# One table preload in the convolution's norm, its steps spaced by one microsecond more, and the sample attention begun at other groups

## The chip, the cores and the metric

The kernel runs on one core of a Trainium2 chip. Five engines work side by side, each through its own list of instructions in order: TensorE (PE, with its weight loads as PEld), VectorE (DVE), ScalarE (ACT), GpSimd (POOL) and SyncE (SP), whose list here is almost only DMA issues. They wait for each other through semaphores. The metric is the device time of one execution in microseconds (us); lower is better.

## The reference

One step of a one-layer streaming encoder, all in f32, for 1024 prompt frames and 32 sample frames (1056 tokens). What matters here:

```
u  = rmsnorm(x) @ w_in                       # gives GLU input, q, k, v, forget logits, two gates
cu = a * sigmoid(gl)                         # GLU
cy = silu(layernorm(depthwise_conv31(cu))) @ w_conv_pw
ao = attend(q, k, v, logf) @ w_attn_o        # softmax(q k^T / 8 + decay), causal, 8 heads of 64
mixed = sigmoid(g_conv) * cy + sigmoid(g_attn) * ao
h  = x + mixed @ w_out
h  = h + (silu(z @ w_gate) * (z @ w_up)) @ w_down,  z = rmsnorm(h)
y  = rmsnorm(h)
```

The prompt attends to itself in 8 query blocks of 128 rows. The 32 sample frames attend to 1024 cached keys and to themselves.

## The kernel before

All activations stand feature by token: a tile has 128 features on the partitions and the 1056 tokens in three chunks of 352 columns. Each f32 operand is split into a high and a low part, so a product of a weight block with a chunk is three matmuls for each of the 128-row steps of the contraction (`products`, line 429). Weight blocks come in by DMA (`raw`), ACT writes the high part (line 245), POOL or DVE the low part (line 248).

**The middle of the program (about 250 to 663 us)** is one long list of PE products, the dense products of line 429 (k, q, v, then the gates, then in `mixers` the convolution's pointwise product), into which the attention is woven. Every four dense matmuls `tick` advances a planner's clock (`plan.pe`) and lets a set of Python generators (threads) put their next piece into the PE list when the planner's clock has reached the time that they yielded. The order on PE is therefore the order of the program text; the tile framework's scheduler orders ACT, DVE, POOL and SP in this region by priority and dependence. The threads are

- `score_thread`, `transpose_thread`, `value_thread`: 32 groups (4 head pairs `p`, 2 heads `hh`, 4 groups `g` of 256 query rows), each with scores (line 1073), softmax (DVE 1080, ACT exp 1083, DVE 1085), transposes of the probabilities (PE 1095, ACT 1102, DVE 1104) and the value product (PE 1112);
- `norm_conv`: the layer norm of the convolution's output, four accumulators of 128x1056, with its sums on PE (line 786), `Ln` on ACT (815), `Exp` (820), `Tanh` (839), and at the end the split operands written to a DRAM scratch `ccd`;
- `sample_thread`: two halves (heads 0 to 3, heads 4 to 7) of the sample attention, `sample_attention(u)`. Each loads the cached keys (`kr`) and values (`vr`) and the decay rows (`ls`) on SP's queue, transposes the keys on PE (line 251), and makes scores (1241, 1243), softmax (1245 to 1249), transposes and value products (1274, 1275), whose results DVE copies to `os` (1278). A half begins when the transposes of so many groups are in the list: 30 for the first half, 28 for the second.

PSUM: the scores have one buffer (`ps`), the transposes, the norm's sums and the sample attention share two banks (`pt`).

**The handover at 663 us.** After `mixers` all tiles of this region are given up and `tokens_in_pairs` lays new pools over the same memory. `attn_out` then issues its loads on SP in this order: `o` for two column blocks (line 1442), the gate `gd` of three output blocks for the first two column blocks (line 1450), `o` for the other two, the `md` of the three blocks, `gd` and `md` of the second half, and then the next two weight blocks `raw` of `w_attn_o` (line 1393). The first product blocks 0 and 1 have their weights already; block 2 needs the first of these `raw` loads. Each load into a new tile waits until the last user of the old tile in that place is done.

Of the kernel before, what the change touches and what calls it, by code (L numbers as in the profile page):

```python
# [37 lines left out]
N_C = 55  # L38
SLACK = 0.65
LOOK = 1  # L40
LATE = 6

CONV_RATE, FORGET_RATE, NORM_RATE = 0.5, 0.25, 0.35
# [20 lines left out]
def f32(ap):  # L64
    return ap.bitcast(F32)
# [75 lines left out]
class Builder:  # L141
# [227 lines left out]
    def jobs(self):  # L369
# [4 lines left out]
        for t in range(4):  # L374
            win(512 + P * t)
            win(P * t)
        assert LATE <= 8
        gates = [(s, j) for s in range(2) for j in range(8)]
        self.early, self.late = gates[:16 - LATE], gates[16 - LATE:]
        gate = lambda s, j: win((W_GC, W_GA)[s] + P * j)  # L380
# [396 lines left out]
    def norm_conv(self):  # L777


        nc, acc, plan = self.nc, self.acc, self.plan  # L780
        self.acc = None
        cs = lambda c: slice(CH * c, CH * c + CH)

        def summed(a, c):
            ps = self.pst()
            nc.tensor.matmul(ps[:, :CH], self.ones, a[:, cs(c)], start=True, stop=True)
            return ps[:, :CH], plan.on_pe(0.62)

        yield plan.pe
        a = self.U([T], s="ln")  # L790
        for t in range(1, 4):
            nc.vector.tensor_add(a, acc[0] if t == 1 else a, acc[t])
            e = plan.on_dve(plan.pe, 1.3)
            yield plan.pe + 2.0
        for c in range(NCH):
            yield max(plan.ready(e), plan.t_next())
            ps, at = summed(a, c)
            for t in range(4):
                nc.vector.scalar_tensor_tensor(acc[t][:, cs(c)], ps, -1.0 / DC, acc[t][:, cs(c)], op0=ALU.mult,
                                               op1=ALU.add)  # L800
            plan.t_used(plan.on_dve(at, 2.1))
            yield plan.pe + 4.0
        a, b = self.U([T], s="ln"), self.U([T], s="sq")
        for t in range(4):
            nc.scalar.activation(b if t else a, acc[t], AF.Square)
            e = plan.on_act(plan.pe, 1.2)
            if t:
                nc.vector.tensor_add(a, a, b)
                e = plan.on_dve(e, 1.3)
            yield plan.pe + 3.0  # L810
        r = b
        for c in range(NCH):
            yield max(plan.ready(e), plan.t_next())
            ps, at = summed(a, c)
            nc.scalar.activation(r[:, cs(c)], ps, AF.Ln, bias=self.eps_ln, scale=1.0 / DC)
            nc.scalar.activation(a[:, cs(c)], ps, AF.Identity, bias=self.eps_ln, scale=1.0 / DC)
            plan.t_used(plan.on_act(at, 1.1))
            yield plan.pe + 2.0

        nc.scalar.activation(r, r, AF.Exp, scale=-0.5)  # L820
        plan.on_act(plan.pe, 1.2)
        yield plan.pe + 2.0
        nc.vector.scalar_tensor_tensor(a, a, -0.5, r, op0=ALU.mult, op1=ALU.mult)
        plan.on_dve(plan.pe, 1.3)
        yield plan.pe + 2.0
        nc.vector.tensor_mul(a, a, r)
        plan.on_dve(plan.pe, 1.3)
        yield plan.pe + 2.0
        nc.vector.scalar_tensor_tensor(r, a, 1.5, r, op0=ALU.add, op1=ALU.mult)
        plan.on_dve(plan.pe, 1.3)  # L830
        del a, b
        yield plan.pe + 2.0
        for t in range(4):
            nc.vector.scalar_tensor_tensor(acc[t], acc[t], self.g("ln_g", t), r, op0=ALU.mult, op1=ALU.mult)
            plan.on_dve(plan.pe, 1.3)
            yield plan.pe + 3.0

            th = self.U([T], s="sg")
            nc.scalar.activation(th, acc[t], AF.Tanh, bias=self.lnb2[:, t:t + 1], scale=0.5)
            nc.scalar.activation(acc[t], acc[t], AF.Identity, bias=self.g("ln_b", t))  # L840
            plan.on_act(plan.pe, 2.3)
            yield plan.pe + 3.0
            nc.vector.scalar_tensor_tensor(acc[t], th, 1.0, acc[t], op0=ALU.add, op1=ALU.mult)
            plan.on_dve(plan.pe, 1.3)
            yield plan.pe + 2.0
            hi, lo = self.U([T], FR, "cch"), self.U([T], FR, "ccl")
            nc.scalar.activation(hi, acc[t], AF.Copy, scale=0.5)
            nc.vector.scalar_tensor_tensor(lo, acc[t], 0.5, f32(hi), op0=ALU.mult, op1=ALU.subtract)
            plan.on_dve(plan.on_act(plan.pe, 1.1), 1.3)
            for i, x in enumerate((hi, lo)):  # L850
                nc.sync.dma_start(self.ccd[t, i], f32(x))
            acc[t] = th = hi = lo = None
            yield plan.pe + 3.0


    def forget_products(self):
# [176 lines left out]
    def attention(self):  # L1033
        nc = self.nc
# [93 lines left out]
        N, plan = len(items), self.plan  # L1128
        o_free = [0.0]
        loaded, probs, pt_ready, pts, done = {}, {}, {}, {}, {"t": 0, "v": 0}  # L1130

        def score_thread():
            for n in range(N):
                p, hh, g = items[n]
                while not (self.c_done and self.ready.get(p)) or n > done["t"] + LOOK:
                    yield None
# [50 lines left out]

        def sample_thread():
            for u in range(2):
                while done["t"] < (30, 28)[u] or not self.ready.get(2 * u + 1):  # L1190
                    yield None
                yield from self.sample_attention(u)

        self.norm = Thread(self.norm_conv())
        self.threads = [Thread(x()) for x in (value_thread, transpose_thread, score_thread, sample_thread)] + [self.norm]

    def sample_attention(self, u):

        nc, I = self.nc, self.I
# [17 lines left out]
                                    channel_multiplier=1)  # L1217
        plan = self.plan
        vr_at = 0.0
        yield plan.pe + 6.0  # L1220
        kT = []
        for i in range(2):
            kT.append(self.U([NP], s="kT"))
            for s in range(2):
                yield plan.t_next()
                t = self.pst()
# [27 lines left out]
        for a in range(2):  # L1254
            yield max(plan.ready(e), plan.t_next())
            t = self.pst()
# [6 lines left out]
        t = self.pst()  # L1263
# [859 lines left out]
```

## Time and profile before

| | |
|---|---|
| median of 3 runs | 1569.53 us (1568.97 to 1569.88) |
| the profiled execution | 1572.19 us |
| its span from the first to the last instruction | 1570.4 us |
| PE busy | 1513.8 us, 96% of the span |
| mean granted TensorE clock | 0.985 of full speed |

The profiled execution is 1.79 us longer than its span (launch and end), and 2.66 us longer than the median of the runs. In the rows below `<-` before an engine name is what ended an idle time; `pd<-cch,wlo` names the output and the inputs of an instruction without buffer numbers; x3 means three instructions in a row.

### The profile page before, as it was taken

The page shows a single profiled execution, that of the slowest core. Times are in us where ns is not written, and L with a number is a line of the kernel's source. Part 1 is how long each engine was busy: PE and PEld are TensorE (multiplying, and loading weights), DVE is VectorE, ACT ScalarE, POOL GpSimd, SP SyncE. Part 2 cuts the span into 40 slices and gives each one's busy share as a digit, 9 for nine tenths or more (in the row PEclk, how much of TensorE's full clock was granted, in tenths as well). Part 3 has the DMA queues.
Part 4 walks back from the last instruction along what each step waited for, and adds up shares of the span by engine and source line. Part 5 has one row for each costly group of instructions (what it writes and reads, how often), then busy time and mean ns, then how long its engine had stood idle before and what let it go on. Part 6 is the DMA issues. An engine that isn't in the chain of part 4 may idle for free.

```text
span 1570.4 us, 27321 instructions
## 1 busy us (share of the span) xinstructions
PE 1513.8 (96%) x10622; PEld 1477.1 (94%) x10622; DVE 957.5 (61%) x1743; ACT 593.2 (38%) x1219; POOL 482.1 (31%) x482
## 2 busy tenths in 40 slices
PE   8999999989999999988998999999999999999997
PEld 7999998979999998888997999999999999999996
DVE  7799998668776566355797544444444444234236
ACT  4411212375655444233543333333333342122115
POOL 2200000433432212310000655565555553122222
PEclk9999999999999999989999999999999999999999
DMA  8312232434633467856854222222222237223213
GB/s 251 120 41 81 87 100 75 132 76 134 203 105 112 119 208 223 266 185 184 262 151 159 82 80 70 71 75 82 82 82 82 82 102 232 83 79 112 84 63 111
DMA packets 212880, 193.54 MB, mean 123 GB/s; under 512 B 13018, under 2 KB 185846, under 8 KB 212751
## 3 DMA queue, kind: packets, MB, share of 16 engines
q1 hardware_dynamic: 212015, 189.91, 39.6%
q8 instruction: 83, 1.36, 0.4%
q0 software_dynamic: 576, 1.62, 0.3%
q14 instruction: 46, 0.38, 0.1%
q10 hardware_dynamic: 160, 0.27, 0.0%
HBM read 135.08 MB, written 56.68 MB: 122 GB/s over the span
## 4 chain that ended last, share of the span: by engine, by line
PE 65%; DVE 6%; ACT 3%; issue 3%; DMA 2%; POOL 1%; SPq 0%; DVEq 0%; ACTq 0%; POOLq 0%
PE pd L1736 26%; PE pd L1430 18%; PE pd L429 11%; PE po L1112 2%; PE ps L1073 2%; PE pt L1095 2%; PE pd L1899 1%; PE pt L251 1%; DVE gate L1495 1%; DMA xt<-xT 1%; DVE h L1659 1%; DVE ml L1499 1%; PE pd L1924 1%; DVE wlo L1418 1%; PE pt L1274 0%
## 5 line engine op out<-in xcount | busy, mean ns | idle before, releaser
L1736 PE MATMUL pd<-zh,whl 128*128 128x264 f32 x2464 | 455.6, 286 | 10.5 <-ACT t L1740 9.6
L1736 PEld LDWEIGHTS pd<-zh,whl 128*128 128x128 f32 x2464 | 386.3, 190 | 11.5 <-ACT t L1740 10.1
L1736 PE MATMUL pd<-zl,whl 128*128 128x264 f32 x1232 | 352.4, 286 | 0.0
L429 PE MATMUL pd<-xl,whi 128*128 128x352 f32 x832 | 270.6, 325 | 0.5 <-POOL xl L539 0.5
L429 PE MATMUL pd<-xh,whi 128*128 128x352 f32 x832 | 271.0, 326 | 0.0
L429 PE MATMUL pd<-xh,wlo 128*128 128x352 f32 x832 | 270.9, 326 | 0.0
L1736 PEld LDWEIGHTS pd<-zl,whl 128*128 128x128 f32 x1232 | 234.3, 190 | 0.0
L1726 DVE TENSOR_TENSOR t<-pd,t 128x264 f32<-128x264 f32 x176 | 75.4, 429 | 202.1 <-POOL t L1744 154.1
L248 POOL TENSOR_TENSOR whl<-ws,whl 128x512 fp32r<-128x512 f32 x105 | 135.6, 1292 | 147.9 <-ACT whl L245 147.9
L429 PEld LDWEIGHTS pd<-xl,whi 128*128 128x128 f32 x832 | 156.8, 188 | 2.0 <-POOL xl L539 0.8
L429 PEld LDWEIGHTS pd<-xh,whi 128*128 128x128 f32 x832 | 156.8, 188 | 1.4
L429 PEld LDWEIGHTS pd<-xh,wlo 128*128 128x128 f32 x832 | 156.8, 188 | 0.7
L766 DVE SCALAR_TENSOR_TENSOR acc<-cu,wdw,acc 128x1024 f32<-128x1024 f32 x120 | 147.3, 1284 | 0.2
L1875 DVE TENSOR_TENSOR h<-pd,h 128x352 f32<-128x352 f32 x96 | 49.7, 523 | 138.3 <-PE pd L1430 138.2
L1430 PE MATMUL pd<-hl,whi 128*128 128x352 f32 x360 | 116.1, 323 | 0.0
L1430 PE MATMUL pd<-hh,whi 128*128 128x352 f32 x360 | 116.1, 322 | 0.0
L1430 PE MATMUL pd<-hh,wlo 128*128 128x352 f32 x360 | 116.1, 322 | 0.0
L245 ACT CAST whl<-ws 128x512 fp32r<-128x512 f32 x115 | 71.4, 621 | 74.7 <-DVE ws L1705 72.1
L248 POOL TENSOR_TENSOR wlo<-raw,whi 128x1024 fp32r<-128x1024 f32 (+1 forms) x31 | 63.9, 2062 | 100.3 <-ACT whi L245 84.7
L245 ACT CAST whi<-raw 128x1024 fp32r<-128x1024 f32 (+1 forms) x47 | 45.0, 957 | 112.0 <-PE pd L429 79.2
L1418 POOL TENSOR_TENSOR wlo<-raw,whi 128x640 fp32r<-128x640 f32 x24 | 39.4, 1643 | 131.9 <-ACT whi L1417 117.0
L1743 POOL TENSOR_TENSOR t<-t,t 128x264 f32<-128x264 f32 x44 | 34.0, 773 | 146.3 <-ACT t L1740 146.3
(349 smaller groups left out, 3061.1 us busy)
## 6 DMA issues: line engine op xcount, KB each, us to landing
raw<-in_w_in SPq DMA_DIRECT2D x35, 512.0 KB, 4.0
hidd<-y SPq DMA_DIRECT2D x43, 264.0 KB, 2.0
hid<-hidd SPq DMA_DIRECT2D x18, 528.0 KB, 4.5
gd<-gate SPq DMA_DIRECT2D x48, 176.0 KB, 1.8
q<-qd SPq DMA_DIRECT2D x32, 256.0 KB, 5.0
raw<-in_w_down SPq DMA_DIRECT2D x24, 320.0 KB, 3.3
raw<-in_w_gate SPq DMA_DIRECT2D x13, 512.0 KB, 4.9
raw<-in_w_up SPq DMA_DIRECT2D x13, 512.0 KB, 4.7
```

The lines of the kernel that those rows point to most:

```text
L245: nc.scalar.copy(hi, src)
L248: (lo_engine or nc.gpsimd).tensor_tensor(lo, src, f32(hi), ALU.subtract)
L429: nc.tensor.matmul(ps[:, :n], lhs, b, start=(m == 0), stop=(m == total - 1))
L766: nc.vector.scalar_tensor_tensor(acc[:, 0:NP], cu[:, j:j + NP], w(j), acc[:, 0:NP], op0=ALU.mult, op1=ALU.add)
L1073: nc.tensor.matmul(s[:, 512 * j:512 * j + e - o], q[:, m, qs], k[:, o:e], start=(m == 0), stop=(m == 1))
L1095: nc.tensor.transpose(t[:, o:o + P], lt[n, b][:, P * kb:P * kb + P], self.ident)
L1418: low = lambda engine: engine.tensor_tensor(lo, r, f32(hi), ALU.subtract)
L1430: self.nc.tensor.matmul(ps[:, :n], a[:, k, :], b, start=(m == 0), stop=(m == total - 1))
L1726: add = lambda out, a, b, op=ALU.add: nc.vector.tensor_tensor(out, a, b, op)
L1736: nc.tensor.matmul(banks[b], x[:, k, :], z[:, k, :], start=first and k == m == 0, stop=i not in copies and k == 3 and m == 2, skip_group_c ...
L1743: nc.gpsimd.tensor_tensor(t2, t2, t5, ALU.add)
L1875: nc.vector.tensor_add(s, ps[:, :CH], s)
```

## The change

Four edits. A preload of the function table `natural_log_exp_and_others` stands ahead of the norm's three `Ln` steps, and the planner's ACT time is advanced by 1.3 us there and at the first `Tanh`. Every fixed pause between the norm's pieces is one microsecond of planner time longer. The pause between the sample attention's loads and its first transposes goes from 6 to 8 us. The first half of the sample attention begins when 22 groups are transposed and no longer 30; the second stays at 28, which was reached when the first half was done, and now is a condition of its own.

```
+SAMPLE = (22, 28)
...
@@ norm_conv
             e = plan.on_dve(plan.pe, 1.3)
-            yield plan.pe + 2.0
+            yield plan.pe + 3.0
...
-            yield plan.pe + 3.0
+            yield plan.pe + 4.0
         r = b
+
+        nc.scalar.preload_act_table_set("natural_log_exp_and_others")
+        plan.on_act(plan.pe, 1.3)
         for c in range(NCH):
             yield max(plan.ready(e), plan.t_next())
             ps, at = summed(a, c)
             nc.scalar.activation(r[:, cs(c)], ps, AF.Ln, bias=self.eps_ln, scale=1.0 / DC)
             nc.scalar.activation(a[:, cs(c)], ps, AF.Identity, bias=self.eps_ln, scale=1.0 / DC)
             plan.t_used(plan.on_act(at, 1.1))
-            yield plan.pe + 2.0
+            yield plan.pe + 3.0
...
             th = self.U([T], s="sg")
+            if t == 0:
+                plan.on_act(plan.pe, 1.3)
             nc.scalar.activation(th, acc[t], AF.Tanh, bias=self.lnb2[:, t:t + 1], scale=0.5)
...
@@ sample_thread
-                while done["t"] < (30, 28)[u] or not self.ready.get(2 * u + 1):
+                while done["t"] < SAMPLE[u] or not self.ready.get(2 * u + 1):
...
@@ sample_attention
-        yield plan.pe + 6.0
+        yield plan.pe + 8.0
```

The diff adds six lines above `Ln`, so line 815 of before is 819 after, 1083 is 1089, 1430 is 1436.

**ACT, the program's first instructions.** Before:

```order
L294 DMA row_100<-in_norm_mix_g 8x128
L326 ACT_TABLE_LOAD
L326 ACTIVATE s_147<-eps_rms 128x1
L245 CAST whi_183<-raw_104 128x512
L489 ACTIVATE junk_203,s_179<-x_108 128x1024
```

After:

```order
L295 DMA row_100<-in_norm_mix_g 8x128
L327 ACT_TABLE_LOAD
L327 ACTIVATE s_147<-eps_rms 128x1
L814 ACT_TABLE_LOAD
L246 CAST whi_183<-raw_104 128x512
L490 ACTIVATE junk_203,s_179<-x_108 128x1024
```

The preload (line 814) waits for nothing, and the scheduler puts it fourth in ACT's list, some 190 rows ahead of the norm. A second new load stands 20 rows on, ahead of the square root of line 259 (258 before), which needs the table of line 327 back.

**ACT, the norm's first two `Ln` steps** (`l` is a softmax tile of the attention, `sq` and `ln` are the norm's). Before:

```order
L1083 ACTIVATE l_3401,s_3408<-l_3401,s_3407 128x1024
L815 ACT_TABLE_LOAD
L815 ACTIVATE sq_3191<-pt_3434,eps_ln 128x352
L816 ACTIVATE ln_3190<-pt_3434,eps_ln 128x352
L1083 ACT_TABLE_LOAD
L1083 ACTIVATE l_3448,s_3455<-l_3448,s_3454 128x896
L1120 COPY otmp_3477<-po_3368 64x256
L815 ACT_TABLE_LOAD
L815 ACTIVATE sq_3191<-pt_3480,eps_ln 128x352
L816 ACTIVATE ln_3190<-pt_3480,eps_ln 128x352
```

After:

```order
L1089 ACTIVATE l_3419,s_3426<-l_3419,s_3425 128x1024
L819 ACT_TABLE_LOAD
L819 ACTIVATE sq_3233<-pt_3457,eps_ln 128x352
L820 ACTIVATE ln_3232<-pt_3457,eps_ln 128x352
L246 CAST whi_3493<-raw_3028 128x1024
L986 COPY kf_3347<-pd_3388 128x352
L1126 COPY otmp_3508<-po_3374 64x256
L1089 ACT_TABLE_LOAD
L1089 ACTIVATE l_3469,s_3476<-l_3469,s_3475 128x896
L819 ACT_TABLE_LOAD
L819 ACTIVATE sq_3233<-pt_3511,eps_ln 128x352
L820 ACTIVATE ln_3232<-pt_3511,eps_ln 128x352
```

The table loads between `Ln` and the attention's `Exp` are the same. Over the whole norm there are six of them before and six after; the whole list has 13 before and 15 after.

**PE, the last rows ahead of the handover** (`pd` is the last chunk of the last block of `mixers`, twelve matmuls; 1274 and 1275 are the value products of the sample attention's second half). Before:

```order
L429 MATMUL pd_7416<-ccl_6457,whi_7284 128x352
L429 MATMUL pd_7416<-cch_6456,wlo_7285 128x352
L429 MATMUL pd_7416<-cch_6460,whi_7284 128x352
L429 MATMUL pd_7416<-ccl_6461,whi_7284 128x352
L1274 MATMUL pt_7425<-pT_7344,vr_7273 128x64 x8
L1275 MATMUL pt_7425<-pT_7410,vs 128x64
L1274 MATMUL pt_7437<-pT_7344,vr_7311 128x64 x8
L1275 MATMUL pt_7437<-pT_7410,vs 128x64
L429 MATMUL pd_7416<-cch_6460,wlo_7285 128x352
L429 MATMUL pd_7416<-cch_6464,whi_7284 128x352
L429 MATMUL pd_7416<-ccl_6465,whi_7284 128x352
L429 MATMUL pd_7416<-cch_6464,wlo_7285 128x352
```

After:

```order
L430 MATMUL pd_7441<-cch_6564,wlo_7357 128x352
L430 MATMUL pd_7441<-cch_6568,whi_7356 128x352
L430 MATMUL pd_7441<-ccl_6569,whi_7356 128x352
L430 MATMUL pd_7441<-cch_6568,wlo_7357 128x352
L430 MATMUL pd_7441<-cch_6572,whi_7356 128x352
L430 MATMUL pd_7441<-ccl_6573,whi_7356 128x352
L430 MATMUL pd_7441<-cch_6572,wlo_7357 128x352
L1436 MATMUL pd_7535<-oh_7516,whl_7520 128x264
```

The sample attention's last value products stand 4 dense matmuls ahead of the handover before and 124 after, and the last rows after are dense products alone. SP's second `gd` load of the handover waits in both programs for a place that a conv operand leaves: by the semaphore value in the built program this is the row with `ccl_6457` before (the first one shown, 25 matmuls ahead of line 1430) and the row with `cch_6568,wlo_7357` after (the fourth shown, 3 matmuls ahead of line 1436).

## Rows read from the trace of the kernel before

**Rows 1.** The page's head and its part 1: busy time of each engine.

```profile
span 1570.4 us, 27321 instructions
PE 1513.8 (96%) x10622; PEld 1477.1 (94%) x10622; DVE 957.5 (61%) x1743; ACT 593.2 (38%) x1219; POOL 482.1 (31%) x482
```

**Rows 2.** Stretches: length, busy PE, PEld, DVE, ACT, POOL, granted clock, DMA share, GB/s.

```profile
310.00:366.00 56.00, 46.35 (x293) 42.33 (x292) 40.12 (x82) 38.11 (x74) 16.51 (x23) 1.00 0.26 70
366.00:600.00 234.00, 230.61 (x1543) 224.52 (x1542) 161.94 (x380) 128.04 (x283) 71.44 (x107) 0.99 0.53 158
663.00:690.00 27.00, 20.51 (x119) 18.92 (x120) 13.70 (x21) 5.73 (x9) 6.82 (x5) 0.81 0.47 170
```

**Rows 3.** Waits of PE, 310 to 366 us: us in total, times, longest.

```profile
PE pt L1095 <- DVE l L1085: 3.5, 3, 1.5
PE po L1112 <- DVE pt L1104: 2.4, 2, 1.5
PE pt L1095 <- ACT kt L996: 1.4, 2, 1.0
PE pt L786 <- DVE pt L1104: 1.2, 1, 1.2
PE pt L1095 <- ACT ln L816: 1.1, 1, 1.1
```

**Rows 4.** Timeline of ACT at the first `Ln`: start, duration, instruction.

```profile
333.19 1.28 ACT L815 ACT_TABLE_LOAD   x1
334.49 0.56 ACT L815 ACTIVATE sq<-pt,eps_ln 128x352 f32<-128x352 f32 x1
335.50 1.28 ACT L1083 ACT_TABLE_LOAD   x1
```

**Rows 5.** Timeline of ACT at the program's start.

```profile
5.42 0.62 ACT L245 CAST whi<-raw 128x512 fp32r<-128x512 f32 x1 [2.48 <-DMA raw<-in_w_in]
...
20.39 0.30 ACT L258 ACTIVATE s<-s,eps_rms 128x3 f32<-128x3 f32 x1 [0.85 <-DVE s L491]
```

**Rows 6.** Timeline of DVE beside that square root.

```profile
20.34 2.25 DVE L259 TENSOR_SCALAR s<-s,eps_rms 128x3 f32<-128x3 f32 x1
...
22.50 0.16 DVE L260 RECIPROCAL s<-s 128x3 f32<-128x3 f32 x1
```

**Rows 7.** Waits of PE, 600 to 663 us.

```profile
PE pt L251 <- DVE pt L1104: 2.0, 2, 1.1
PE ps L1241 <- DVE s L1080: 0.4, 1, 0.4
```

**Rows 8.** Timeline of SP's queue at the handover.

```profile
656.89 0.81 SPq L1450 DMA_DIRECT2D gate<-gd  x2
...
659.04 3.55 SPq L1450 DMA_DIRECT2D gate<-md  x3
...
665.61 2.47 SPq L1393 DMA_DIRECT2D raw<-in_w_attn_o  x2
```

**Rows 9.** Stretches around the handover, columns as in group 2.

```profile
657.00:659.00 2.00, 2.00 (x19) 1.93 (x18) 0.00 (x0) 2.00 (x4) 0.35 (x1) 1.00 0.44 48
659.00:673.00 14.00, 8.95 (x49) 7.56 (x48) 5.55 (x9) 2.51 (x4) 4.23 (x3) 0.88 1.07 388
```

**Rows 10.** DMA issues, 656 to 673 us: count, KB each, us to landing.

```profile
gate<-md SPq DMA_DIRECT2D x6, 264.0 KB, 5.1
gate<-gd SPq DMA_DIRECT2D x5, 264.0 KB, 4.4
```

**Rows 11.** Timeline of PE at the handover.

```profile
662.24 0.32 PE L429 MATMUL pd<-cch,wlo 128*128 128x352 f32 x1
...
669.87 0.32 PE L1430 MATMUL pd<-oh,whl 128*128 128x264 f32 x1
673.42 0.59 PE L1430 MATMUL pd<-oh,whl 128*128 128x264 f32 x1 [3.23 <-ACT whl L1417]
```

**Rows 12.** Timeline of ACT: the weights of output block 2.

```profile
672.75 0.62 ACT L1417 CAST whl<-raw 128x512 fp32r<-128x512 f32 x1 [9.64 <-DMA raw<-in_w_attn_o]
```

More of the change, by code (lines that the diff above doesn't have):

```diff
@@ L40 @@
 LOOK = 1
+SAMPLE = (22, 28)
 LATE = 6
@@ L793, in norm_conv @@
             e = plan.on_dve(plan.pe, 1.3)
-            yield plan.pe + 2.0
+            yield plan.pe + 3.0
         for c in range(NCH):
@@ L809, in norm_conv @@
                 e = plan.on_dve(e, 1.3)
-            yield plan.pe + 3.0
+            yield plan.pe + 4.0
         r = b
+        nc.scalar.preload_act_table_set("natural_log_exp_and_others")
+        plan.on_act(plan.pe, 1.3)
         for c in range(NCH):
@@ L817, in norm_conv @@
             plan.t_used(plan.on_act(at, 1.1))
-            yield plan.pe + 2.0
+            yield plan.pe + 3.0
         nc.scalar.activation(r, r, AF.Exp, scale=-0.5)
         plan.on_act(plan.pe, 1.2)
-        yield plan.pe + 2.0
+        yield plan.pe + 3.0
         nc.vector.scalar_tensor_tensor(a, a, -0.5, r, op0=ALU.mult, op1=ALU.mult)
         plan.on_dve(plan.pe, 1.3)
-        yield plan.pe + 2.0
+        yield plan.pe + 3.0
         nc.vector.tensor_mul(a, a, r)
         plan.on_dve(plan.pe, 1.3)
-        yield plan.pe + 2.0
+        yield plan.pe + 3.0
         nc.vector.scalar_tensor_tensor(r, a, 1.5, r, op0=ALU.add, op1=ALU.mult)
@@ L831, in norm_conv @@
         del a, b
-        yield plan.pe + 2.0
+        yield plan.pe + 3.0
         for t in range(4):
@@ L835, in norm_conv @@
             plan.on_dve(plan.pe, 1.3)
-            yield plan.pe + 3.0
+            yield plan.pe + 4.0
             th = self.U([T], s="sg")
+            if t == 0:
+                plan.on_act(plan.pe, 1.3)
             nc.scalar.activation(th, acc[t], AF.Tanh, bias=self.lnb2[:, t:t + 1], scale=0.5)
@@ L841, in norm_conv @@
             plan.on_act(plan.pe, 2.3)
-            yield plan.pe + 3.0
+            yield plan.pe + 4.0
             nc.vector.scalar_tensor_tensor(acc[t], th, 1.0, acc[t], op0=ALU.add, op1=ALU.mult)
             plan.on_dve(plan.pe, 1.3)
-            yield plan.pe + 2.0
+            yield plan.pe + 3.0
             hi, lo = self.U([T], FR, "cch"), self.U([T], FR, "ccl")
@@ L852, in norm_conv @@
             acc[t] = th = hi = lo = None
-            yield plan.pe + 3.0
+            yield plan.pe + 4.0
     def forget_products(self):
@@ L1189, in sample_thread @@
             for u in range(2):
-                while done["t"] < (30, 28)[u] or not self.ready.get(2 * u + 1):
+                while done["t"] < SAMPLE[u] or not self.ready.get(2 * u + 1):
                     yield None
@@ L1219, in sample_attention @@
         vr_at = 0.0
-        yield plan.pe + 6.0
+        yield plan.pe + 8.0
         kT = []
```

## The prediction

> **What bounds the kernel now.** I read the page's head first: PE is busy for 1513.8 of 1570.4 us [rows 1]. No instruction on PE is added or taken away (both programs have the same count of each line's matmuls), so the change can only move the some 57 us in which PE is idle, and the time that PE runs at a low clock. Next the stretches: the norm stands at 310 to 366 us, where PE is busy for 46.35 of 56 us, 9.65 us idle; in the 234 us behind it only 3.4 us are idle; and at the handover, 663 to 690 us, 6.5 of 27 us are idle and the granted clock is 0.81 [rows 2]. The reader is to see that two short stretches hold over a quarter of PE's idle time, and that the change touches both. Then who is waited for. In the norm the sum of PE's waits is 9.6 us, spread over DVE's softmax and probability splits and ACT's copies, none longer than 1.5 us [rows 3]: these are attention pieces that come late since ACT and DVE have the norm's pieces ahead of them. At the handover one wait stands out: 3.23 us for the high weights of output block 2 [rows 11], and ACT, which makes them, waited 9.64 us for a DMA, the `raw` load [rows 12]. So the handover is bound by the load that stands last in SP's list, and DMA is full from 659 to 673 us (share 1.07, 388 GB/s) while it was hardly used in the two us ahead of that (48 GB/s) [rows 9].
>
> **The preload.** It is meant to spare the switches between `Ln` and `Exp`. One costs 1.28 us of ACT, and the `Ln` starts 0.02 us behind it [rows 4]; five spared switches would be 6.4 us of ACT. But the lists of the two programs show the six loads of the norm in both: the preload was put at the program's start, where it does nothing for the norm. Its gain is 0. Its cost there: it runs behind line 326, whose work ends 2.48 us ahead of the cast at 5.42 us, which waits for a DMA [rows 5]; 1.28 us fit in. The load that it makes necessary ahead of line 258 can start when ACT is free, 0.85 us ahead of 20.39 us, and end at 20.82, so the root ends at 21.1 us. Its reader on DVE, line 260, runs at 22.50 us since DVE's own line 259 takes 2.25 us [rows 6]. Even with the load begun at 20.39 us the root would end at 21.97 us. Cost 0; both bounds 0, and the cover is 0.5 us at the least; without it PE would wait for up to 1.3 us at the first diagonal product.
>
> The Trainium skill (ScalarE: Activation LUTs, section What ACT_TABLE_LOAD costs) says that each switch costs 1283 ns and a drain of some 1380 ns more, 2.66 us together. The trace agrees with the first number alone: no such drain stands between load and `Ln`. By the page the first new load would end at 5.6 us, 0.2 us past the start of that cast, and the sum would be larger by at most that.
>
> **The norm's pauses.** One microsecond of planner time is one or two ticks, four to eight dense matmuls more between pieces, with nothing added. What it can spare is DVE's part of the waits, where two or three of the norm's 1.3 us pieces stood in a row: of the 9.6 us [rows 3] 5.9 us are waits for softmax and split results (3.5 and 2.4). The `Ln` steps do not follow these pauses alone but the planner's time for the sums and the PSUM banks, and in the list after each reload of the `Exp` table now stands behind one cast and two copies more, so the waits for ACT stay or move. I take -1.2 us; -5 (half of all) to +2 us (a few more waits of the usual 1 us each, since the pieces now reach further into the attention).
>
> **The sample attention.** Loads, transposes and products are the same; they move on SP, PE, ACT, DVE and POOL from behind group 30 to group 22, and the second half from behind the attention to its last groups. Before they cost PE 2.4 us of waits, for PSUM banks and for the single score buffer [rows 7], all at the first half; the second ran beside dense products alone. After, both halves have the attention beside them: in the list only four transposes stand between an attention score and the first half's scores, which use the same buffer. I found no load on SP that is held up so far that its reader would come late. I take +0.6 us; -2.4 (all gone) to +3 us (each half with as much again as the first has now).
>
> **The handover.** This is the term that decides. SP issues in order. Its second `gd` load waits for a conv operand's place, and everything behind it, 11 halves of 264 KB [rows 10], two `o` of about 528 KB and then `raw`, waits with it. Before it got through at 656.89 us [rows 8], 5.67 us ahead of the end of `mixers` (662.24 + 0.32 = 662.56 us, [rows 11]), since 25 matmuls still followed, 18 of them the sample attention's value products. After, these products are long done, and only three dense matmuls follow, about 0.5 us. So the same chain of loads starts 5.67 - 0.5 = 5.2 us later against the end of `mixers`. What is on the path: the loads up to `raw` are about 4.25 MB, 11 us at 388 GB/s [rows 9]; before, 15.8 us went by from 656.89 us to the cast at 672.75 us [rows 8, 12]. If DMA alone sets this, the cast and PE's block 2 come 5.2 us later. If SP's issue sets it, the shift is smaller: before, the three `md` issues took 3.55 us, where two `gd` issues take 0.81 us, so about 2.2 us were a wait, for the sample's last product, which after is gone; `raw` would be issued 3.0 us later. PE reaches the gap at the same distance from the end of `mixers` (its blocks 0 and 1 end at 669.87 + 0.32 us), so nothing hides a part: the wait is already 3.23 us long and grows. DMA was full throughout, so I take 4.6 us, in bounds of 3.0 and 5.2. What lies behind starts from PE's products and moves along. The clock was 0.81 here over 27 us, some 10 us at the half level, so some 5 us lost [rows 2]; the wait is longer, but the clock was already low behind it, and I take this as unchanged, within 1.7 us either way, a third of that loss.
>
> The Trainium skill (DMA: Bandwidth & Descriptors, section Bandwidth) gives 425 GB/s for a large transfer, above the 388 GB/s of the row. By its figure 4.25 MB would take 10.0 us, an estimate by which this term would be about 1 us smaller; the rest of the sum stays.
>
> **The sum.** 0 - 1.2 + 0.6 + 4.6 = +4.0 us. The profiled execution would take 1572.19 + 4.0 = 1576.2 us; it stands 2.66 us above the median of the runs, so the forecast is 1569.53 + 4.0 = 1573.5 us. A measurement of this kernel tells a change from none at about 0.2%, 3.1 us: slower by 0.25%.
>
> **The rivals.** *The handover's loss is paid by the norm* (1569.5 us): the pauses take away 4 to 5 us of the 9.6 us in the norm. For it speaks that most waits there are about 1 us, the size of the added pause; against it that the table loads between `Ln` and `Exp` stay and that a pause of the planner does not move the `Ln` steps. *The norm's waits go altogether* (1564.5 us, faster): 9.6 us less, 4.6 us more. It decides for faster once 7.7 of the 9.6 us are gone. It would be so if the waits came from pieces in a row alone; the ACT waits of 2.5 us [rows 3] speak against it. *The sample halves get in the attention's way* (1577.5 us): PE waits at both for banks and scores, 3 us more where I took 0.6, and a low clock follows one of them, 1.7 us. For it speaks the single score buffer; against it that a half has only some ten places at which it needs one. That the change doesn't do what its words say is part of the forecast: the preload brings nothing. The Trainium skill (ScalarE: Activation LUTs, section Table sets) names that set as the one in which `Ln` after `Exp` needs no second load; were it in force in the norm, five loads of 1.28 us would go and the norm's waits with them, which is the rival of 1564.5 us. The order after excludes it as a cause.
>
> **How the numbers follow.** The forecast 0.47, paid by the norm 0.25, norm's waits gone 0.15, sample in the way 0.13. The forecast's own range is 1571 to 1576 us (handover 3.0 to 5.2, clock 1.7, the rest small); a fifth of it lies within 0.2%. Slower: 0.38 of the forecast's 0.47 and 0.12 of the last case, 0.50. Within 0.2%: 0.09, 0.22 of the second case, 0.01 of the last, 0.32. Faster: the third case and 0.03 of the second, 0.18. The range reaches from the better part of the second case to the last one, 1567 to 1578 us; most of the third case is left out below, and little above.
>
> **What would show it.** After: 15 table loads, the fourth ACT instruction one of them, PE's start unchanged at the first diagonal product (right: preload 0). SP's second `gd` issue of the handover about 0.5 us before the last dense matmul ends, ACT's cast of block 2 some 14 to 15 us behind that end (before 10.2), PE's wait there 6 to 8.5 us. PE's waits in the norm 6 to 10 us, at the two sample halves 2 to 5 us. I am wrong if the wait at block 2 is below 5 us, if the norm's waits fall below 5 us, or if a wait stands in the attention that I have not listed.

## The result, and the profile after

The changed kernel takes 1589.57 us (median of four runs, 1588.24 to 1591.53), the kernel before 1569.70 us in the same comparison: ratio 1.0129, 95% interval 1.0112 to 1.0145, some 20 us slower. The forecast was 4 us slower, and the time lies 11.6 us above the range. The profiled execution took 1591.53 us, 19.3 us more than that of before.

The head of its page: PE has 3.6 us more of busy time than in [rows 1] for the same 10622 matmuls, and the span is 19.4 us longer, so nearly 16 us are idle PE.

```profile
span 1589.8 us, 27335 instructions
PE 1517.4 (95%) x10622; PEld 1480.6 (93%) x10622; DVE 963.1 (61%) x1743; ACT 595.2 (37%) x1221; POOL 483.0 (30%) x482
```

PE executes the same number of matmuls in both, so the start of its n-th matmul can be compared between two traces. Each column below is one stretch of the program and tells by how many us the difference against before grew in it; a positive number is time lost. Matmul n = 1600 starts at 264 us of before, 2400 at 399, 3000 at 490, 4000 at 644, 4200 at 684, the last at 1561. The kernels other than the change are the experiments below.

```
                          start   norm  400-490  490-644  handover  rest   all
n up to                    1600   2400     3000     4000      4200  last
the change                 -0.8    8.6      3.2      1.9       6.5   0.0  19.4
e2 pauses +1 alone          0.3    8.1      3.3     -2.3      -1.7  -2.0   5.8
e10 pauses +0.5             0.6    3.1      3.1      0.4       2.8   0.1  10.1
e11 pauses +2               0.2   -3.0     13.1      5.9       3.0  -1.8  17.4
e3 preload alone           -0.5    0.7     -1.1     -0.8      -0.9  -1.4  -4.1
e1 sample 22, 28           -0.5    0.0      0.0     14.5       5.3  -1.4  17.9
e12 sample 22, 31           0.3    0.0      0.0      1.8       3.4  -1.8   3.7
e4 change, sample 22, 32   -1.2    8.6      1.0      0.6       7.1  -1.3  14.9
e5 change, preload placed   0.3   -0.6      1.1      3.9       4.5  -1.0   8.1
e7 change, raw first        0.4    7.9      1.1      3.3       1.9  -2.1  12.5
e6 before, preload placed  -0.4   -6.1     -0.3      0.0      -0.4  -3.4 -10.5
e8 before, raw first       -1.0    0.0      0.0      0.0      -5.5  -2.3  -8.7
e9 before, both            -0.1   -6.2     -0.3     -1.5      -5.8  -2.5 -16.3
```

These are single executions. A step of 1.5 us either way that turns up near 735 us with no difference ahead of it belongs to none of the edits: the profiled executions of the change and of before have a stretch at the lower clock there, most of the others have none. So a sum here can differ by a few us from the medians, which decide. Where an edit moves the order on PE, the n-th matmul is not the same instruction in both: of the change's 6.5 us in the handover column, 0.5 lie ahead of the end of `mixers`. And the column named norm ends at 399 us of before, while the norm's last ACT piece starts at 417 us in before, at 451 us in the change and at 469 us in e11, so a longer norm reaches into the next column.

The change lost time at three places: in the norm, near 470 us, and at the handover. The norm first. PE's waits from 310 to 380 us, to be held against [rows 3] (us in total, times, longest):

```profile
PE pt L1101 <- DVE l L1091: 4.6, 2, 2.5
PE pt L252 <- ACT ln L820: 3.1, 1, 3.1
PE po L1118 <- DVE pt L1110: 2.2, 3, 1.0
PE pt L252 <- DVE pt L1110: 2.0, 1, 2.0
PE po L1118 <- ACT pt L1108: 1.5, 1, 1.5
```

They sum to 13.4 us where before had 9.6. More than the sum, their length changed: before had none over 1.5 us, now four are 2 us or more. The stretches behind three of these, and behind the wait at 466.62 us (length, busy PE, PEld, DVE, ACT, POOL, granted clock, DMA share, GB/s):

```profile
317.00:321.00 4.00, 3.84 (x17) 3.68 (x18) 2.80 (x8) 2.42 (x6) 0.10 (x1) 0.58 0.79 223
344.50:349.50 5.00, 4.89 (x24) 4.47 (x25) 1.12 (x3) 1.84 (x4) 0.00 (x0) 0.66 0.41 116
375.00:379.00 4.00, 3.95 (x17) 3.76 (x18) 1.98 (x6) 0.59 (x1) 1.72 (x3) 0.50 0.35 107
466.60:471.50 4.90, 4.88 (x26) 4.81 (x26) 2.57 (x7) 1.99 (x4) 0.81 (x3) 0.65 0.28 85
```

PE is busy there, but at a granted clock of 0.50 to 0.66, so mostly at the lower of its two levels, 1.2 instead of 2.4 GHz; in [rows 2] the norm has a clock of 1.00. The waits cost again in the work behind them: the stretch with the norm is 8.6 us longer with 3.8 us more of waits.

Where the 3.1 us wait comes from is read on ACT:

```profile
339.69 1.28 ACT L1089 ACT_TABLE_LOAD   x1
340.99 1.04 ACT L1089 ACTIVATE l<-l,s 128x896 f32<-128x896 f32 x1
341.94 0.19 ACT L1089 ACTIVATION_READ_ACCUMULATOR l<-l,s 128x1 f32 x1
342.14 1.28 ACT L819 ACT_TABLE_LOAD   x1
343.43 0.55 ACT L819 ACTIVATE sq<-pt,eps_ln 128x352 f32<-128x352 f32 x1
343.89 0.55 ACT L820 ACTIVATE ln<-pt,eps_ln 128x352 f32<-128x352 f32 x1
```

Line 820 is the last reader of the norm's sum in a `pt` bank, for which the key transposes (`kf`) wait until 344.49 us. The sum itself was ready some 5 us earlier (its two matmuls start at 338.26 us). In between, ACT loads the table for an attention `Exp`, runs it, and loads the table for `Ln`: of those 5 us, 2 x 1.28 are table loads. These are switches that the preload in the norm's text was to spare, and did not.

Near 470 us, behind the norm's last piece, the moved order put another step ahead of its neighbour. DVE:

```profile
462.73 2.49 DVE L990 CAST k<-kf 64x320 fp32r<-64x320 f32 x2 [1.26 <-ACT kf L986]
465.25 0.72 DVE L995 COPY ksf<-kf 128x32 f32<-128x32 f32 x1
465.89 1.21 DVE L1110 TENSOR_TENSOR pt<-pt,pt 128x512 fp32r<-128x512 f32 x3
```

The end of a dense key block puts 3.2 us of casts and copies on DVE just ahead of the attention's probability split (line 1110), which holds a `pt` bank; the key transposes wait 2.58 us for that bank.

The handover: SP, PE and ACT, as [rows 8, 11, 12] showed them before.

```profile
675.47 0.33 SPq L1456 DMA_DIRECT2D gate<-gd  x1
...
681.84 3.95 SPq L1456 DMA_DIRECT2D gate<-md  x3
686.20 1.06 SPq L1399 DMA_DIRECT2D raw<-in_w_attn_o  x2
```

```profile
675.60 0.32 PE L430 MATMUL pd<-cch,wlo 128*128 128x352 f32 x1
...
692.49 0.59 PE L1436 MATMUL pd<-oh,whl 128*128 128x264 f32 x1 [9.13 <-ACT whl L1423]
```

```profile
691.82 0.62 ACT L1423 CAST whl<-raw 128x512 fp32r<-128x512 f32 x1 [10.61 <-DMA raw<-in_w_attn_o]
```

The held `gd` issue, the second of three, now comes 0.45 us before `mixers` ends (675.60 + 0.32 = 675.92 us), where it came 5.67 us before. The `raw` issue stands 10.3 us behind that end (3.05 before): the held issue is 5.2 us later, and SP waits 3.2 us on the way for `o` loads issued earlier, most of it between the three `md` issues, which take 3.95 us (1.45 before). The cast stands 15.9 us behind the end of `mixers` (10.2 before), and PE waits 9.13 us instead of 3.23.

### The profile page after: what moved, and what is told of

It is laid out like the page before. It is cut to its first block, busy times and chain, and to the rows that moved or that the text cites. A ratio compares the mean times of both kernels' runs of the same rounds, so it can differ in the third digit from the quotient of the medians.

```text
span 1589.8 us, 27335 instructions
## 1 busy us (share of the span) xinstructions
PE 1517.4 (95%) x10622; PEld 1480.6 (93%) x10622; DVE 963.1 (61%) x1743; ACT 595.2 (37%) x1221; POOL 483.0 (30%) x482
## 4 chain that ended last, share of the span: by engine, by line
PE 80%; DVE 7%; issue 4%; ACT 4%; DMA 3%; POOL 1%; SPq 1%; DVEq 0%; ACTq 0%; POOLq 0%
PE pd L1742 26%; PE pd L430 24%; PE pd L1436 18%; PE po L1118 2%; PE ps L1079 2%; PE pt L1101 2%; PE pd L1905 1%; PE pt L252 1%; DVE gate L1501 1%; SPq L475 1%; DVE h L1665 1%; DVE ml L1505 1%; DVE l L1091 1%; PE pd L1930 1%; DMA gate<-md 1%
## 5 line engine op out<-in xcount | busy, mean ns | idle before, releaser
L1742 PE MATMUL pd<-zh,whl 128*128 128x264 f32 x2464 | 454.8, 286 | 11.6 <-ACT t L1746 10.8
L767 DVE SCALAR_TENSOR_TENSOR acc<-cu,wdw,acc 128x1024 f32<-128x1024 f32 x120 | 147.1, 1274 | 0.2
L1063 POOL TENSOR_SCALAR_AFFINE_SELECT cr<-cr 128x128 f32<-128x128 f32 x64 | 25.6, 400 | 179.5 <-DVE s L1086 90.3
```

What stands on the lines that cost most here:

```text
L767: nc.vector.scalar_tensor_tensor(acc[:, 0:NP], cu[:, j:j + NP], w(j), acc[:, 0:NP], op0=ALU.mult, op1=ALU.add)
L1742: nc.tensor.matmul(banks[b], x[:, k, :], z[:, k, :], start=first and k == m == 0, stop=i not in copies and k == 3 and m == 2, skip_group_c ...
```

## The experiments

The kernel before was run again beside each set of experiments; its medians there lie between 1568.64 and 1569.86 us, and each ratio below is against the kernel before of its own set.

**The edits one at a time.** Each is put alone into the kernel before. The sample attention's edit:

```
+SAMPLE = (22, 28)
...
-                while done["t"] < (30, 28)[u] or ...
+                while done["t"] < SAMPLE[u] or ...
...
-        yield plan.pe + 6.0
+        yield plan.pe + 8.0
```

> The kernel before with the sample attention's edit alone: begin at groups 22 and 28, pause of 8 us. Theory A (each edit has its own place and price, and they add): the norm and the stretch up to 600 us stay as before; the wait for the weights of output block 2 is 8 to 10 us as in the changed kernel (3.23 before), and the kernel is 6 to 8 us slower, 1576 to 1578 us. Rival B (the late loads of the handover come from the norm's drift as much as from the sample halves): the wait stays below 5 us and the time within 3 us of before.

Measured: 1588.81 us, ratio 1.0115 (1.0095 to 1.0135). The norm's column is 0.0, and the wait at output block 2 is 9.30 us, as theory A has it, so rival B falls; but the edit costs 19 us and not 6 to 8. In the table 5.3 us of it are the handover and 14.5 us the stretch of 490 to 644 us, where the change itself lost 1.9. PE's longest waits there, from 600 us:

```profile
PE pt L252 <- DMA kr<-in_cache_k: 3.1, 1, 3.1
PE ps L1242 <- DVE s L1081: 1.5, 1, 1.5
PE pt L252 <- DVE s L1085: 1.5, 1, 1.5
PE pt L252 <- DVE pt L1105: 1.1, 1, 1.1
```

The longest is for a DMA, the second half's cached keys. SP and the loads from 599 to 608 us (count, KB each, us to landing):

```profile
600.41 1.46 SPq L1207 DMA_DIRECT2D kr<-in_cache_k  x2
```

```profile
kr<-in_cache_k SPq DMA_DIRECT2D x2, 512.0 KB, 9.0
```

They were issued at 600.4 us, behind conv operand, gate, weight and `q` loads; DMA moved 295 GB/s from 599 to 608 us with its engines busy throughout (share 1.12). They were wanted at 604.1 us, where the wait begins. In the change the same pair was issued at 607.79 us and wanted at 614.77, and there was no wait. From 490 to 600 us the edit alone has 3.7 us of waits at the first half, where before had 1.6; the run with 31 groups below has the same 3.7.

The pauses alone, and the preload with its two planner entries alone:

```
-            yield plan.pe + 2.0
+            yield plan.pe + 3.0
...
```

One fixed pause of the norm is left as it was, in the change too: the 4.0 us behind each of the first three sums.

> The kernel before with the longer pauses of the norm alone, no preload, sample attention as before. Theory A: the time lost in the norm and behind it (some 8 us by 400 us, 4 to 5 us more around 470 us) comes from the pauses: 8 to 13 us slower, 1578 to 1583 us, the wait at output block 2 as before (3.2 us). Rival C (the planner's 1.3 us of ACT time that come with the preload move the norm into the dense blocks' ends): within 4 us of before, 1566 to 1574 us.

Measured: 1580.01 us, ratio 1.0061 (1.0045 to 1.0078). The loss in the norm and near 470 us is that of the change, nearly wait for wait (2.10, 3.10, 1.47, 2.35 and 1.78 us in the norm, 2.60 us at the key transposes near 467 us). The handover is not worse than before.

```
+        nc.scalar.preload_act_table_set("natural_log_exp_and_others")
+        plan.on_act(plan.pe, 1.3)
...
+            if t == 0:
+                plan.on_act(plan.pe, 1.3)
```

> The kernel before with the preload and the two planner entries of 1.3 us on ACT alone. Two table loads more at the program's start; PE's first products not late. Theory A: the planner's entries change little, within 3 us of before. Rival C: most of the loss in the norm is here, 6 to 13 us slower.

Measured: 1568.20 us, ratio 0.9991 (0.9979 to 1.0003): no change. So rival C falls, and the loss in the norm is the pauses'. That the edits add, as theory A had it, falls too: 10 and 19 us alone, 20 together. The sample attention's edit has two parts, the groups and the pause of 8 us; they were not tried apart.

**The second half later.** In the changed kernel:

```
-SAMPLE = (22, 28)
+SAMPLE = (22, 32)
```

> The changed kernel with the second half of the sample attention begun at group 32 instead of 28, the first at 22. If the lost cover at the handover is the second half's value products, which in the kernel before stood among the last dense products, then they stand there again: wait at output block 2 back to 3 to 5 us, and 5 to 7 us faster than the changed kernel, 1583 to 1585 us. If the handover's loss hangs on the first half or on the norm, the wait stays at 8 to 9 us and the time at 1588 to 1591 us.

Measured: 1588.10 us, the wait at block 2 7.19 us and a new one of 3.76 us at the first product. The forecast failed: now the first `o` loads, at the head of SP's list, wait for the sample attention's value products (SP's longest wait, 8.4 us). So a second half begun early and one begun late both meet a load that waits to take over an old tile's place.

> The kernel before with the sample attention begun at groups 22 and 31 (22 and 28 in the change), pause 8 us, norm as before. In the built program SP's second gate load still waits for a matmul 3 ahead of the handover, as with 28, though the second half's value products stand 68 dense matmuls from it, no longer 148. If that place in memory sets the handover, the wait for output block 2 stays at 8 to 10 us. The 3.1 us wait for the kr load near 607 us belongs to the second half begun early: it goes, with the low clock behind it, and the kernel is 4 to 8 us faster than with 28, 1581 to 1585 us. If the first half begun early is what costs, 1587 to 1590 us.

(The edit is the first one, with 31 for 28.) Measured: 1575.85 us, ratio 1.0045 (1.0030 to 1.0060). The wait at block 2 stays at 8.25 us with the second half's value products 68 dense matmuls from the end, so it is not these products that decide there. The held gate load comes 0.45 us before the end of `mixers`, as in the change, so what points to the cause is the place of the gate tile. The 3.1 us wait for `kr` is gone, and the stretch of 490 to 644 us costs 1.8 us instead of 14.5: it was the second half, not the first. The time fell by more than expected, 13 us (12 when each is held against its own kernel before).

**The preload in its place.** One call holds the preload behind what stands ahead of it in the text on ACT, behind the norm's squares; first in the changed kernel, then, without the planner's entries, in the kernel before:

```
-        nc.scalar.preload_act_table_set("natural_log_exp_and_others")
+        self.tc.keep_in_program_order(nc.scalar.preload_act_table_set("natural_log_exp_and_others"))
```

> The changed kernel with the preload held at its place in ACT's list, behind the norm's squares (in the changed kernel it stands at the program's start). Built, it has two table loads in the norm instead of six and no new ones at the start; PE's list is the same. Theory P (the waits that the longer pauses bring end on ACT, whose Ln and Exp steps change tables while PE's transposes want the sums' PSUM bank): the 3.1 us wait of the kf transposes for line 820 goes below 1 us and the norm's waits from 13 to 8 to 10 us, 4 to 8 us faster than the changed kernel, 1582 to 1586 us. Rival Q (the waits are set by the place of the attention's pieces in PE's list, with DVE as last releaser): at most 2 us faster, 1587 to 1590 us.

> The kernel before with only the preload, held at its place; planner, pauses and sample attention as before, PE's list the same. Four table loads of 1.28 us go from the norm. By theory P the waits for ACT (2.5 us) and a part of those for DVE's softmax, which wait for the Exp, go: PE's waits in the norm 9.6 to 5 to 7 us, 1564 to 1567 us. By rival Q they stay at 8.5 to 9.6 us, 1568 to 1570 us.

Measured: 1579.97 us, 9.6 us less than the change and more than theory P had; and 1563.49 us, ratio 0.9961 (0.9948 to 0.9973), 5.6 us less than before. PE's waits in the norm, first of the changed kernel with it:

```profile
PE pt L1101 <- DVE l L1091: 4.9, 3, 2.3
PE pt L252 <- DVE pt L1110: 1.9, 1, 1.9
PE po L1118 <- DVE pt L1110: 0.9, 1, 0.9
PE pt L252 <- ACT ln L820: 0.4, 1, 0.4
```

then of the kernel before with it:

```profile
PE pt L1096 <- DVE l L1086: 2.0, 2, 1.3
PE po L1113 <- DVE pt L1105: 1.5, 1, 1.5
PE pt L786 <- DVE pt L1105: 0.9, 1, 0.9
```

Of the change's 13.4 us 8.1 are left and the wait for line 820 is 0.4 us; of before's 9.6 us 4.4 are left, less than theory P had expected. PE's list did not change, so rival Q falls. In the table the norm's column goes from 8.6 to -0.6 in the changed kernel and from 0 to -6.1 in the kernel before: with the switches gone the longer pauses still cost 5.5 us there, and the 2.6 us wait near 467 us stays. In the kernel before the waits for DVE shrank as well: the softmax step there reads what ACT's `Exp` leaves, so who is named last need not be who is late.

**The raw loads first.** At the handover the splits of the first two weight blocks and the two `raw` loads go ahead of the second half's gate loads on SP; in the changed kernel and in the kernel before:

```
         for p in range(2):
+            if p:
+                ws = [self.block() for _ in range(2)]
+                self.fetch(2)
             for j in range(3):
...
         split_o(0)
-        ws = [self.block() for _ in range(2)]
-        self.fetch(2)
         split_o(1)
```

> The changed kernel with SP's order at the handover altered: the two raw loads (and the splits of the first two weight blocks) stand ahead of the six 264 KB gate loads of the second half, no longer behind them. If the wait for output block 2 is set by what stands ahead of its load in SP's list, these 1.6 MB at 388 GB/s are 4.1 us: the wait goes from 9.1 to 4.5 to 6 us, and the kernel is 4 to 7 us faster than the changed one (clock included), 1583 to 1586 us. If it is set by the splits of blocks 0 and 1, whose places the load takes, the wait shrinks by under 1.5 us: 1588 to 1590 us.

> The kernel before with the same alteration of SP's order at the handover. Here the wait is 3.2 us and 3 to 4 us could be taken from the cast: wait 0 to 0.5 us, 3 to 5 us faster, 1565 to 1567 us, a version that beats both. If the splits of blocks 0 and 1 set it: wait 2 to 3 us, 1568 to 1570 us.

Measured: 1584.84 us, 4.7 us less than the change, and 1562.05 us, ratio 0.9947 (0.9930 to 0.9964), 7.1 us less than before, more than expected, though the wait shrank by less. SP and PE in the latter:

```profile
661.93 0.94 SPq L1393 DMA_DIRECT2D raw<-in_w_attn_o  x2
662.93 1.67 SPq L1450 DMA_DIRECT2D gate<-gd  x3
664.95 1.70 SPq L1450 DMA_DIRECT2D gate<-md  x3
```

```profile
667.91 0.39 PE L1430 MATMUL pd<-oh,whl 128*128 128x264 f32 x1 [1.35 <-ACT whl L1417]
```

The wait went from 3.23 to 1.35 us. The third wait ahead of it (0.74 us) is gone and the products between run at full clock, so PE arrives earlier and the wait seems larger than the gain shows. In the changed kernel the same: its wait only went from 9.13 to 8.61 us, outside what was expected of it, while its handover column in the table is 4.6 us lower and its time as expected.

**Both mends.**

> The kernel before with both mends: the preload held at its place in the norm, and the two raw loads ahead of the second half's gate loads. The two lie some 290 us apart and share nothing, so they should add: 5.6 + 7.1 us faster than before, 1555 to 1559 us. If a part of either gain was a shift that the other gives too, 1560 to 1562 us.

Measured: 1556.20 us, ratio 0.9922 (0.9903 to 0.9941), 12.4 us faster than before, where the two alone give 5.6 + 7.1. They add within the interval.

**Half and twice the pauses.** The pauses that the change lengthens by 1 us are longer by 0.5 us, and by 2 us. But these two kernels also alter the pause behind the first three sums, which the change leaves at 4.0 us:

```
e10
-            yield plan.pe + 4.0
+            yield plan.pe + 3.5
e11
-            yield plan.pe + 4.0
+            yield plan.pe + 5.0
```

So they are not the change's edit at half and twice its size, and no order by size can be read from the three runs alone.

> The kernel before with the norm's pauses longer by 0.5 us instead of 1 us, nothing else. Theory D (the loss grows with the pauses, since a longer norm reaches further into the attention): 3 to 7 us slower than before, 1573 to 1577 us. Theory S (the loss comes from single steps that happen to fall on an attention or block-end step, and any change of the pauses draws them anew): no such order; 1563 to 1582 us, with waits at other places than with 1 us.

> The kernel before with the norm's pauses longer by 2 us instead of 1 us. Theory D: 15 to 22 us slower than before, 1584 to 1592 us. Theory S: no such order, 1563 to 1582 us; the 2.6 us wait of the kf transposes near 467 us, which came with 1 us, gone or elsewhere.

Measured: 1580.20 us, ratio 1.0072 (1.0049 to 1.0096), and 1591.32 us, ratio 1.0146 (1.0124 to 1.0169); with 1 us it was 1580.01. Neither theory has this whole. For S: e10 costs as much as 1 us does, 12 us against 10. The norm's columns are +3.1, +8.1 and -3.0 us, but counted on to 490 us, since the longer norm reaches on, they are +6.2, +11.4 and +10.1. With 2 us the key transposes' wait near 467 us is not there, but others are (3.2 us for a softmax result at 470.56 us, and 3.8 us for the `kr` load at 604.22 us). For D: 2 us costs most in all. The handover moved too, with the sample attention's edit left out; PE's wait at block 2 in e10, then in e11:

```profile
PE pd L1432 <- ACT whl L1419: 5.9, 1, 5.9
PE pd L1432 <- ACT whl L1419: 8.0, 1, 8.0
```

In e10 the sample attention's last value products still end 0.8 us before `mixers` does, as in the kernel before. What the runs show is that none of the three kernels with longer pauses gained in sum, and that the place of the loss moves with each.

## Why the prediction was wrong

**The norm's pauses**, -1.2 us with +2 as the far end, is the step that failed. It was priced as a relief of DVE, "with nothing added", and bounded from the waits of before. Measured with the pauses alone: +8.1 us in the norm and +3.3 us near 470 us; in the change 8.6 and 3.2. Of the 15.4 us between the forecast's +4.0 and the trace's +19.4, 13.0 are this term. Two things were missing. A shifted step meets other neighbours: the waits of before were treated as a stock to be taken from, and the order of the changed PE list, in which the new neighbours stood, is read in the prediction at the sample attention's scores and ahead of the handover, but not at the key blocks' ends and the `pt` banks. And the price of a wait was taken as its length; here three of the four of 2 us and more had a stretch at the lower clock behind them. That the pauses cause the loss is shown by the run with them alone. That a part of it hangs on the table switches is shown by the preload in its place (8.6 us in the norm with the switches, 5.5 without). Why the rest falls where it does is read from the traces and was not tried by itself.

**The preload**, 0, was right: the two new loads stand where the order showed them, one as the fourth instruction of ACT, and alone it makes no measurable difference. What the prediction made of it was too little: it saw that the six switches stayed, and did not carry on that the pauses' `Ln` steps would still each hold a `pt` bank through them. Its rival at 1564.5 us has the switches spared and the norm's waits of 9.6 us gone, less 4.6 us lost at the handover. The preload in its place spares four switches, not five, and gives the kernel before 5.6 us; that its 1563.5 us stands near that rival's time is luck, since no loss at the handover is in it. The changed kernel with it takes 1580.0 us. The Trainium skill (ScalarE: Activation LUTs, section Table sets) has one load for `Ln` and then `Exp` in this set; with the preload in its place the trace agrees, one load stands in the whole of the norm's attention work up to the first `Tanh`.

**The sample attention**, +0.6 us (-2.4 to 3): 1.9 us in the change, inside the bounds, though the pauses alone have -2.3 us in the same column. But the sentence that no load is held up so far that its reader comes late did not hold for the edit alone, where the `kr` load came 3.1 us late. The changed kernel was spared this since PE came to the key transposes 7.0 us after the issue and not 3.7; that is read from the two traces and was not tried by itself.

**The handover**, +4.6 us (3.0 to 5.2): right in mechanism, place and chain, too small in size: 6.0 us from the end of `mixers` on. The held load came 5.2 us later against that end, as forecast. From it to the cast went 16.35 us and 15.86 before, so the cast came 5.7 us later and PE's wait grew by 5.9. The upper bound took the same chain to last as long as before; the bound by SP's issues, with `raw` issued 3.0 us later, did not hold, since `raw` was issued 7.2 us later. The stretches from the held issue to the cast, before and after, and the 7.5 us behind the wait, before and after:

```profile
656.90:672.75 15.85, 11.04 (x67) 9.59 (x65) 5.55 (x9) 4.36 (x6) 4.68 (x4) 0.89 0.98 343
675.50:691.80 16.30, 5.70 (x27) 4.77 (x25) 4.79 (x5) 1.93 (x2) 4.23 (x3) 0.73 0.99 336
673.40:680.90 7.50, 6.93 (x32) 6.63 (x33) 2.44 (x4) 0.94 (x1) 1.28 (x1) 0.55 0.21 71
692.50:700.00 7.50, 6.96 (x30) 6.65 (x31) 2.48 (x4) 0.91 (x1) 1.27 (x1) 0.50 0.18 62
```

In the mean DMA was full in both (shares 0.98 and 0.99), at 343 and 336 GB/s. The clock behind the wait was low before too, 0.55 and now 0.50, so taking its cost as unchanged was right within 0.3 us. The reason given for the late start, that the value products among the last matmuls are the cover, is not the whole: with the second half at 31 or 32 groups the wait stays long, and in e10 it grew to 5.9 us with these products in place. What the waits point to is the old tile whose place a held load takes over, and these places are dealt anew by a change of the order ahead; that was not tried by itself.

**The rivals.** None of the three is what happened. *The sample halves get in the attention's way* had the right kind (bank waits and a low clock behind one of them), but with the wrong thread in it, and priced at 4.1 us where the norm and the stretch behind it cost 11.8. The range ended at the sum of the priced places; it had no room for a collision at a place not listed, which the prediction itself named as what would make it wrong.

## What to carry to other kernels

An edit of planner times in a woven program draws all later neighbours anew, so its price is not that of the waits it is meant to ease. Look in the new order for every shared bank and every in-order engine behind the shifted steps, and price a long wait with the slow stretch that may stand behind it. A table preload without inputs stands where the scheduler puts it: look at the engine's list, and tie it to its place. And where a load that holds up PE stands behind loads that are needed later, move it ahead on the queue: here that and the preload in its place made the kernel 12 us faster, while the change made it 20 us slower.

## What the runs showed of the hardware that was not expected

A wait on PE was followed by a stretch at a granted clock of 0.50 to 0.66 of 4 to 7.5 us in the cases shown above, all of them waits of 2 us and more; the norm, with three of them, became 8.6 us longer with 3.8 us more of waiting. But the length of the wait alone does not decide it. With the pauses alone the first of these waits, 2.10 us again, had the full clock behind it; with the sample edit alone two waits of 1.41 and 1.07 us in the norm had the lower clock behind them:

```profile
318.20:322.20 4.00, 3.99 (x29) 3.91 (x30) 2.87 (x7) 3.05 (x8) 0.41 (x1) 1.00 0.86 243
340.50:344.00 3.50, 3.50 (x17) 3.43 (x15) 1.63 (x4) 3.47 (x6) 2.62 (x2) 0.52 0.00 0
```

And loads of 512 KB took 9.0 us to land with the sample edit alone, while DMA moved 295 GB/s in all, against 6.2 us for the same pair in the changed kernel.
